# A 3x3 convolution with 2x2 max pooling: two row algorithms on alternate image pairs, in a hand-written order

## The chip, the core and the metric

The kernel runs on one core of a Trainium2 chip. The core has a matrix engine (TensorE, PE in the profile), a vector engine (VectorE, DVE), a scalar engine (ScalarE, ACT), a general engine (GpSimd, POOL), queues that start DMA transfers (SyncE's is SP), an on-chip memory of 128 partitions (SBUF), and the accumulator memory that TensorE writes (PSUM[...]). The metric is device time in microseconds (us), the median of several executions. The profile's span runs from the first instruction to the last and is about 1 us shorter than that time.

## What is computed

The reference convolves 16 images of 64 channels and 64x64 pixels with 128 filters of 3x3, with zeros around the image, and then takes the maximum of each 2x2 block.

```python
batch, c_in, h, w, c_out, k = 16, 64, 64, 64, 128, 3
x_pad = np.pad(x, ((0, 0), (0, 0), (1, 1), (1, 1)))
conv[b, co] += weight[co, ci, kh, kw] * x_pad[b, ci, kh:kh+h, kw:kw+w]
...
output[b, c, i, j] = np.max(conv[b, c, 2*i:2*i+2, 2*j:2*j+2])
```

The output is 16 x 128 x 32 x 32 in fp32. Both kernels multiply in bf16 and accumulate in fp32.

## The kernel before

Two images make a pair: the 64 channels of the first lie on partitions 0 to 63, those of the second on 64 to 127, and the loop runs over eight pairs. An image pair comes in by two DMA transfers of 1 MB (L66, L67), top half and bottom half, and is cast to bf16 into `xpad` with a zero row above and below: the top half by ScalarE (L72), the bottom half by VectorE (L73), the zero rows by GpSimd (L70, L71).

The weights are prepared once. For each of the nine taps, VectorE copies the tap's weights twice side by side (L52, L53), TensorE transposes them in fp32 (L55), and ScalarE casts the result into `wt` (L57), so that the same 64x128 weights lie on both halves of the partitions.

A pair is worked in eight chunks of eight rows. A chunk has two accumulators, `pa` and `pb`, one PSUM bank for each image. For each of the nine taps there are two matmuls, one for each image: L96 uses partitions 0 to 63, L97 uses 64 to 127. I call the two a *pair of matmuls*. A matmul streams 8 x 64 = 512 columns, or 8 x 63 = 504 for a tap at the left or right edge.

Then, for each image, ScalarE copies the accumulator to SBUF (`sb`, L107), VectorE takes the maximum of neighbouring columns (`cm`, L109) and then of neighbouring rows into `oacc` (L113). The output of a pair goes out in two stores of 512 KB from ScalarE's queue (L101, L122). Tile pools and the framework's scheduler set the order; PSUM has three buffers each for `pa` and `pb`.

Of the kernel before, what the change touches and what calls it, by code (L numbers as in the profile page):

```python
# [1 line left out]

# [5 lines left out]


@with_exitstack
def kernel(
    ctx: ExitStack,
    tc: tile.TileContext,
    x: bass.AP,
    weight: bass.AP,
    pool_size: bass.AP,
    out: bass.AP,
):
    nc = tc.nc  # L20
    FP32 = mybir.dt.float32
    BF16 = mybir.dt.bfloat16

    B, CI, H, W = x.shape
    CO, _, K, _ = weight.shape
    assert pool_size == 2
    HP = H + 2
    WP = W + 2
    HO, WO = H // 2, W // 2

    ROWS = 8
    NCHUNK = H // ROWS

    const = ctx.enter_context(tc.tile_pool(name="const", bufs=1))
    wpsum = ctx.enter_context(tc.tile_pool(name="wpsum", bufs=2, space=bass.MemoryType.PSUM))
    psum = ctx.enter_context(tc.tile_pool(name="psum", bufs=3, space=bass.MemoryType.PSUM))
    xraw_pool = ctx.enter_context(tc.tile_pool(name="xraw_pool", bufs=2))
    xpad_pool = ctx.enter_context(tc.tile_pool(name="xpad_pool", bufs=2))
    colmax_pool = ctx.enter_context(tc.tile_pool(name="colmax_pool", bufs=8))
    oacc_pool = ctx.enter_context(tc.tile_pool(name="oacc_pool", bufs=2))  # L40

    ident = const.tile([128, 128], FP32)
    make_identity(nc, ident)

    wraw = const.tile([CO, CI * K * K], FP32)
    nc.sync.dma_start(out=wraw, in_=weight.rearrange("a b c d -> a (b c d)"))  # L46

    wk = []
    for k in range(K * K):
        wdup = const.tile([CO, 2, CI], FP32, name=f"wdup_{k}")  # L50
        src = wraw.rearrange("a (ci k) -> a k ci", k=K * K)[:, k, :]
        nc.vector.tensor_copy(out=wdup[:, 0, :], in_=src)  # L52
        nc.vector.tensor_copy(out=wdup[:, 1, :], in_=src)  # L53
        wp = wpsum.tile([128, 128], FP32, name="wpsum")
        nc.tensor.transpose(wp, wdup.rearrange("a b c -> a (b c)"), ident)  # L55
        wt = const.tile([128, CO], BF16, name=f"wt_{k}")
        nc.scalar.copy(out=wt, in_=wp)  # L57
        wk.append(wt)

    out_v = out.rearrange("b c h w -> c b (h w)")  # L60

    for p in range(B // 2):
        xv = x[2 * p : 2 * p + 2].rearrange("b c h w -> (b c) h w")
        xraw_t = xraw_pool.tile([128, H // 2, W], FP32, name="xraw_t")
        xraw_b = xraw_pool.tile([128, H // 2, W], FP32, name="xraw_b")
        nc.sync.dma_start(out=xraw_t, in_=xv[:, 0 : H // 2])  # L66
        nc.sync.dma_start(out=xraw_b, in_=xv[:, H // 2 : H])  # L67

        xpad = xpad_pool.tile([128, HP, W], BF16)
        nc.gpsimd.memset(xpad[:, 0, :], 0.0)  # L70
        nc.gpsimd.memset(xpad[:, H + 1, :], 0.0)  # L71
        nc.scalar.copy(out=xpad[:, 1 : 33, :], in_=xraw_t)  # L72
        nc.vector.tensor_copy(out=xpad[:, 33 : H + 1, :], in_=xraw_b)  # L73

        oacc = oacc_pool.tile([128, 2, HO * WO], FP32)

        for c in range(NCHUNK):
            y0 = c * ROWS
            pa = psum.tile([128, ROWS, W], FP32, name="pa")
            pb = psum.tile([128, ROWS, W], FP32, name="pb")  # L80
            korder = [1, 4, 0, 3, 6, 2, 5, 8, 7]
            for i, k in enumerate(korder):
                kh, kw = k // K, k % K
                st = i == 0
                sp = i == K * K - 1
                rows = xpad[:, y0 + kh : y0 + kh + ROWS]
                if kw == 1:
                    mv = rows.rearrange("p a b -> p (a b)")
                    oa, ob = pa, pb
                elif kw == 0:  # L90
                    mv = rows[:, :, 0 : W - 1]
                    oa, ob = pa[:, :, 1:W], pb[:, :, 1:W]
                else:
                    mv = rows[:, :, 1:W]
                    oa, ob = pa[:, :, 0 : W - 1], pb[:, :, 0 : W - 1]
                nc.tensor.matmul(oa, wk[k][0:CI, :], mv[0:CI], start=st, stop=sp)  # L96
                nc.tensor.matmul(ob, wk[k][CI:128, :], mv[CI:128], start=st, stop=sp)  # L97

            for half, pt in ((0, pa), (1, pb)):
                if half == 0 and c == 5:  # L100
                    nc.scalar.dma_start(  # L101
                        out=out_v[:, 2 * p : 2 * p + 2, 0 : HO * WO // 2],
                        in_=oacc[:, :, 0 : HO * WO // 2],
                    )
                pv = pt
                sb = colmax_pool.tile([128, ROWS, W], FP32, name=f"sb{half}")
                nc.scalar.copy(out=sb, in_=pv)  # L107
                cm = colmax_pool.tile([128, ROWS, WO], FP32, name=f"cm{half}")
                nc.vector.tensor_tensor(  # L109
                    out=cm, in0=sb[:, :, 0::2], in1=sb[:, :, 1::2],  # L110
                    op=mybir.AluOpType.max,
                )
                nc.vector.tensor_tensor(  # L113
                    out=oacc.rearrange("p b (h w) -> p b h w", h=HO)[
                        :, half, y0 // 2 : y0 // 2 + ROWS // 2, :
                    ],
                    in0=cm[:, 0::2, :],
                    in1=cm[:, 1::2, :],
                    op=mybir.AluOpType.max,
                )  # L120

        nc.scalar.dma_start(  # L122
            out=out_v[:, 2 * p : 2 * p + 2, HO * WO // 2 :],
            in_=oacc[:, :, HO * WO // 2 :],
        )


# [1 line left out]
_INS = ['x', 'weight', 'pool_size']  # L129
_OUTS = [((16, 128, 32, 32), 'float32')]  # L130
#: Inputs that are plain numbers.
_NUMBERS = {'pool_size': 2}


# [26 lines left out]
```

## Time and profile before

| what | value |
|---|---|
| time, median of 3 | 146.98 us (146.45 to 147.07) |
| span of the profile | 145.9 us |
| bytes read, written | 17.07 MB, 8.39 MB |
| mean granted TensorE clock | 0.995 |
| pairs of matmuls in the convolution | 576 |

"Busy" in the profile is the time in which at least one instruction of an engine was under way. A matmul's record is longer than its turn, since the next one starts before it has drained, so two lines of matmuls that run side by side can each show nearly the whole span. What counts for TensorE is the distance between starts.

### The profile page before, as it was taken

Reading aid. Unit: us, or ns where it says so; the run is one execution under the profiler, and the core shown is the slowest. Engines: PE = TensorE matmul, PEld = TensorE weight load, DVE = VectorE, ACT = ScalarE, POOL = GpSimd, SP = SyncE. Lnnn points to the kernel's source line nnn. Section 1 sums busy time; section 2 is a strip of 40 time slices with the busy share of each in tenths; the row PEclk is TensorE's granted clock in tenths of the full one; section 3 lists DMA queues with packets and bytes.
Section 4 is the critical chain, followed back from the end, with each engine's and each line's share of the span. In section 5 each row is a group of like instructions: output and inputs, shape, how many; then the busy total and the mean of one; then the engine's idle time right before and its main releaser. Section 6 shows DMA issues by size and latency. Waiting matters only on the chain.

```text
span 145.9 us, 3022 instructions
## 1 busy us (share of the span) xinstructions
PE 131.7 (90%) x1161; PEld 58.0 (40%) x1161; DVE 95.2 (65%) x282; ACT 86.2 (59%) x146; POOL 8.6 (6%) x22
## 2 busy tenths in 40 slices
PE   0159999999999999999999999999999999999930
PEld 0023344444444444444444444444444444444410
DVE  0630287686768685878679676867686858586770
ACT  3174644578555955597367755695559555463640
POOL 2000000030001200030003000300002000000000
PEclk9999999999999999999999999999999999999997
DMA  5999995308960598139840994030302112030303
GB/s 164 409 427 427 395 332 231 144 2 236 384 247 3 133 344 334 57 63 284 369 152 16 259 408 184 7 146 0 144 4 84 60 67 81 13 131 4 144 0 144
DMA packets 6813, 25.64 MB, mean 176 GB/s; under 512 B 528, under 2 KB 528, under 8 KB 4752
## 3 DMA queue, kind: packets, MB, share of 16 engines
q1 hardware_dynamic: 2448, 17.07, 32.3%
q10 hardware_dynamic: 4352, 8.39, 15.1%
q8 instruction: 9, 0.15, 0.4%
q14 instruction: 4, 0.03, 0.1%
HBM read 17.07 MB, written 8.39 MB: 175 GB/s over the span
## 4 chain that ended last, share of the span: by engine, by line
PE 90%; DMA 4%; ACT 2%; DVE 1%; SPq 0%; issue 0%; ACTq 0%
PE pa L96 86%; DMA xraw_t<-in_x_dram 4%; PE pb L97 2%; PE wpsum L55 2%; ACT xpad L72 1%; DVE cm L109 1%; ACT sb L107 0%; DVE oacc L113 0%; SPq L46 0%; ACT wt L57 0%; ACTq L107 0%
## 5 line engine op out<-in xcount | busy, mean ns | idle before, releaser
L96 PE MATMUL pa<-xpad,wt 64*128 64x504 bf16 (+1 forms) x576 | 127.6, 382 | 0.0
L97 PE MATMUL pb<-xpad,wt 64*128 64x504 bf16 (+1 forms) x576 | 127.6, 382 | 0.0
L96 PEld LDWEIGHTS <-wt 64*128 64x128 bf16 x576 | 54.8, 95 | 70.5 <-issue 3.6
L109 DVE TENSOR_TENSOR cm<-sb 128x256 f32<-128x256 f32 x128 | 53.6, 423 | 35.9 <-ACT sb L107 35.9
L107 ACT COPY sb<-pa 128x512 f32<-128x512 f32 x64 | 37.5, 585 | 46.2 <-PE pb L97 33.0
L97 PEld LDWEIGHTS <-wt 64*128 64x128 bf16 x576 | 54.8, 95 | 0.5 <-issue 0.5
L113 DVE TENSOR_TENSOR oacc<-cm 128x128 f32<-128x128 f32 x128 | 36.8, 292 | 3.9
L107 ACT COPY sb<-pb 128x512 f32<-128x512 f32 x64 | 37.9, 592 | 0.0
L72 ACT CAST xpad<-xraw_t 128x2048 bf16<-128x2048 f32 x8 | 15.3, 1909 | 4.9 <-DMA xraw_t<-in_x_dram 4.9
L70 POOL MEMSET xpad<- 128x64 bf16 x8 | 7.5, 937 | 101.2 <-DVE oacc L113 101.2
L73 DVE CAST xpad<-xraw_b 128x2048 bf16<-128x2048 f32 x8 | 9.8, 1226 | 3.4 <-DMA xraw_b<-in_x_dram 3.4
L55 PE MATMUL wpsum<-ident,wdup 128*128 128x128 f32 x9 | 3.5, 452 | 8.3 <-ACT wt L57 4.2
L71 POOL MEMSET xpad<- 128x64 bf16 x8 | 7.3, 918 | 0.0
L55 PEld LDWEIGHTS wpsum<-ident,wdup 128*128 128x128 f32 x9 | 1.6, 187 | 10.4 <-ACT wt L57 6.2
L52 DVE COPY wdup<-wraw 128x64 f32<-128x64 f32 x9 | 1.9, 209 | 3.7 <-DMA wraw<-in_weight_dram 3.7
L57 ACT CAST wt<-wpsum 128x128 bf16<-128x128 f32 x9 | 2.2, 265 | 3.1 <-PE wpsum L55 3.1
L53 DVE COPY wdup<-wraw 128x64 f32<-128x64 f32 x9 | 1.9, 208 | 0.0
L72 ACT ACT_TABLE_LOAD x1 | 1.3, 1283 | 0.7 <-PEq L142 0.7
masks.py:199 POOL TENSOR_SCALAR_AFFINE_SELECT ident<-ident 128x128 f32<-128x128 f32 x1 | 0.3, 292 | 0.0
masks.py:197 POOL MEMSET ident<- 128x128 f32 x1 | 0.2, 204 | 0.3 <-POOLq L142 0.3
L142 POOL MEMSET const-float32-0.0<- 128x1 f32 x1 | 0.1, 98 | 0.2 <-issue 0.2
L142 POOL MEMSET const-bfloat16-1.0<- 128x1 bf16 x1 | 0.1, 101 | 0.0
(2 smaller groups left out, 0.2 us busy)
## 6 DMA issues: line engine op xcount, KB each, us to landing
xraw_t<-in_x_dram SPq DMA_DIRECT2D x8, 1024.0 KB, 8.5
xraw_b<-in_x_dram SPq DMA_DIRECT2D x8, 1024.0 KB, 7.0
out_dram<-oacc ACTq DMA_DIRECT2D x16, 512.0 KB, 3.1
wraw<-in_weight_dram SPq DMA_DIRECT2D x1, 288.0 KB, 2.9
```

The source lines that it names most:

```text
L52: nc.vector.tensor_copy(out=wdup[:, 0, :], in_=src)
L55: nc.tensor.transpose(wp, wdup.rearrange("a b c -> a (b c)"), ident)
L57: nc.scalar.copy(out=wt, in_=wp)
L70: nc.gpsimd.memset(xpad[:, 0, :], 0.0)
L71: nc.gpsimd.memset(xpad[:, H + 1, :], 0.0)
L72: nc.scalar.copy(out=xpad[:, 1 : 33, :], in_=xraw_t)
L73: nc.vector.tensor_copy(out=xpad[:, 33 : H + 1, :], in_=xraw_b)
L96: nc.tensor.matmul(oa, wk[k][0:CI, :], mv[0:CI], start=st, stop=sp)
L97: nc.tensor.matmul(ob, wk[k][CI:128, :], mv[CI:128], start=st, stop=sp)
L107: nc.scalar.copy(out=sb, in_=pv)
L109: nc.vector.tensor_tensor(out=cm, in0=sb[:, :, 0::2], in1=sb[:, :, 1::2], op=mybir.AluOpType.max,)
L113: nc.vector.tensor_tensor(out=oacc.rearrange("p b (h w) -> p b h w", h=HO)[:, half, y0 // 2 : y0 // 2 + ROWS // 2, :], in0=cm[:, 0::2, :], ...
```

## The change

Both new algorithms compute the two rows of a 2x2 block together, to need fewer products than the six row products (two output rows by three weight rows) of the direct form. Let g0, g1, g2 be the three rows of a filter (each with its three horizontal taps), and x-1, x0, x1, x2 the four input rows under two output rows e and o.

The eight image pairs alternate. On the even ones, "K", there are **five** row products:

- A = (g2-g1) x1 + g0 x-1, B = (g0-g1) x0 + g2 x2, and R = g1 (x0+x1); then e = A + R, o = B + R, so max(e, o) = max(A, B) + R.
- TensorE makes A (step `PA`) and B (`PB`); ScalarE copies A to SBUF (`EV`); VectorE writes max(A, B) over B in PSUM (`MX`); TensorE adds R on top of it (`PR`); ScalarE copies the odd columns (`OD`) and VectorE takes the maximum with the even columns, reading PSUM with a step of two (`CM`). VectorE makes x0+x1 (`KS`).

On the odd ones, "W", there are **four**:

- M = (g0-g1+g2)/2 times (x1-x0), P = (g0+g1+g2)/2 times (x0+x1), g0 (x-1 - x1) and g2 (x2 - x0); e = M + P + g0(..), o = -M + P + g2(..).
- TensorE makes M (`P2`); ScalarE writes -M into a second accumulator (`SE`); TensorE adds g0(..) to the first (`P0`) and g2(..) to the second (`P3`); `ev` and `mx` take the maximum of the two as above; P is added on top (`P1`); `od` and `cm` end it. VectorE makes x0+x1 (`WS`), GpSimd the three differences (`Z`, `Y`, `E`, the first five `E` on VectorE).

A quarter of an image pair (8 pooled rows) is the unit of work, and there are 16 quarters of each kind. Four accumulators of two banks, one for each image, fill PSUM. The K pairs are loaded and cast to bf16 by GpSimd's own DMA queue; the W pairs stay fp32. The weights are combined and transposed in bf16 at the start (steps `T..`, `V..`), and eight matmuls on constants stand ahead of everything. The order of all steps on all engines is written out:

```diff
+    ctx.enter_context(tc.manual_schedule())
+    acc = [psum.tile([128, 2, R, W], FP32, name=f"acc_{i}") for i in range(4)]
...
+    def pa(i):
+        taps(t, D2, step2(kx[j], 2 * q * R + 1), start=True)
+        taps(t, G0, step2(kx[j], 2 * q * R - 1), skip=0 if q == 0 else None)
...
+    def rowmax(g, h=None):
+        t = acc[tb[g]][:, halves(h)]
+        nc.vector.tensor_tensor(out=t, in0=t, in1=ev[g][:, halves(h)], op=MAX)
+    def odd(g, h=None):
+        nc.scalar.copy(out=od[g][:, halves(h)], in_=acc[tb[g]][:, halves(h), :, 1::2])
...
+    def colmax(g, h=None):
+        nc.vector.tensor_tensor(
+            out=o, in0=acc[tb[g]][:, s, :, 0::2], in1=od[g][:, s], op=MAX
+        )
...
+    def on_gpsimd(inst):
+        behind(inst, sbuf_op[0])
...
+    STEADY = """
+        PA+0 OD-1 CM-1 P2+0 mx-1 EV+0 PB+0 SE+0 P1-1 MX+0 P0+0 od-1 P3+0 cm-1 ev+0 PR+0 KS+1
+        WS+1 Z+1 Y+1 E+2
+    """
+    TAIL = """
...
+        ev.15.1 mx.15.1 P1.14 od.14 cm.14 PR.15 OD.15 CM.15 P1.15.0 P1.15.1
+        od.15.0 cm.15.0 od.15.1 cm.15.1
+    """
```

`on_gpsimd` makes each of GpSimd's row operations wait for the last row operation of VectorE (`KS`, `WS`, ...). The last product (`P1.15`), its `od`, `cm` and store are done image by image, the two stores on two queues.

## Prediction

> **What bounds the kernel now.** I read the busy shares first, then the chain of work that ended last, then the costliest groups.
>
> ```profile
> PE 131.7 (90%) x1161; PEld 58.0 (40%) x1161; DVE 95.2 (65%) x282; ACT 86.2 (59%) x146; POOL 8.6 (6%) x22
> ...
> PE 90%; DMA 4%; ACT 2%; DVE 1%; SPq 0%; issue 0%; ACTq 0%
> ...
> L96 PE MATMUL pa<-xpad,wt 64*128 64x504 bf16 (+1 forms) x576 | 127.6, 382 | 0.0
> L97 PE MATMUL pb<-xpad,wt 64*128 64x504 bf16 (+1 forms) x576 | 127.6, 382 | 0.0
> ...
> L109 DVE TENSOR_TENSOR cm<-sb 128x256 f32<-128x256 f32 x128 | 53.6, 423 | 35.9 <-ACT sb L107 35.9
> L107 ACT COPY sb<-pa 128x512 f32<-128x512 f32 x64 | 37.5, 585 | 46.2 <-PE pb L97 33.0
> ```
>
> TensorE is 90% of the span and of the chain; ScalarE and VectorE wait for it. L96 and L97 each show 127.6 us because they run side by side. The timeline gives the pace:
>
> ```profile
> 137.69 0.38 PE L96 MATMUL pa<-xpad,wt 64*128 64x512 bf16 x1
> 137.69 0.38 PE L97 MATMUL pb<-xpad,wt 64*128 64x512 bf16 x1
> ...
> 139.63 0.38 PE L96 MATMUL pa<-xpad,wt 64*128 64x512 bf16 x1
> ...
> 140.10 0.58 ACT L107 COPY sb<-pa 128x512 f32<-128x512 f32 x1 [0.87 <-PE pb L97]
> ```
>
> Nine pairs in 1.94 us: 0.216 us a pair, for 504 columns as for 512. So 576 x 0.216 = 124.4 us. The last turn ends at 139.85; 139.85 - 124.4 = 15.4 us is what the start costs (first weights, input[...]), and 145.9 - 139.85 = 6.05 us is the tail. Also: ScalarE starts 0.25 us after the end of the turn that it waits for.
>
> [...]early pairs stand 0.43 us apart, until about 18 us:
>
> ```profile
> 14.43 0.63 PE L96 MATMUL pa<-xpad,wt 64*128 64x504 bf16 x1
> ...
> 14.86 0.63 PE L96 MATMUL pa<-xpad,wt 64*128 64x504 bf16 x1
> ```
>
> [...]a memset that takes 0.15 us at the start takes 1.20 us beside a 1.23 us cast and ends with it.[...]
>
> ```profile
> 46.77 1.23 DVE L73 CAST xpad<-xraw_b 128x2048 bf16<-128x2048 f32 x1
> 46.89 1.20 POOL L70 MEMSET xpad<- 128x64 bf16 x1 [14.29 <-DVE oacc L113]
> ```
>
> [...]
>
> **The matmuls.** A K quarter has five products of three taps, 15 pairs; a W quarter has 12. So 16 x 27 = 432 pairs, 432 x 0.216 = 93.3 us. In 24 of them one row of eight falls away at an image edge (-0.65 us), and the last product, image by image, runs its three pairs as six single turns (+0.65). Net 93.3 us, 31.1 less than before. I take 0.216 for the row patterns with a step of two as well, since lines of 63 and 64 values already cost the same.
>
> **Prices of the rest.** ScalarE: the 512-value copy has 585 ns, 592 beside it, and a 128-value cast 265, so 0.83 ns a value: 1024 values 1.02 us (`EV`, `SE`, `ev`), 512 values 0.59 (`OD`, `od`). Sum of a round: 3 x 1.02 + 2 x 0.59 = 4.2 us. VectorE: 256 values 423 ns, 128 values 292, so 1.02 ns a value; two in a row stand 0.33 us apart for 256[...]; the full duration I estimate at 1.25 us for `MX`, `mx` and 0.72 for `CM`, `cm`[...]. [...]`WS` 0.59.[...] GpSimd: no two-input operation is in the trace.[...]
>
> TensorE's round is 27 x 0.216 = 5.83 us: every other engine has less work, so TensorE stays the bound if the order lets it.
>
> **Does it?** I walk one round from `STEADY`, t = 0 at `PA`'s start. Turns on TensorE: `PA` 0-1.30, `P2` -1.94, `PB` -3.24, `P1` of the round before -3.89, `P0` -4.54, `P3` -5.18, `PR` -5.83.
> ScalarE: `OD` of the round before waits for `PR`, 0.25 to 0.84; `EV` waits for `PA`, 1.55 to 2.57; `SE` follows, 2.60 to 3.62, and `P0` needs it at 3.89; `od` 4.14 to 4.73; `ev` 4.79 to 5.81.
> VectorE: `CM` 0.88 to 1.60, and `PB`, which reuses its accumulator, needs it at 1.94; `mx` 1.5 to 2.8, `P1` needs it at 3.24; `MX` waits for `PB`, 3.5 to 4.75, `PR` needs it at 5.18; `cm` 4.78 to 5.5, the next `PA` needs it at 5.83; `KS`, `WS` then to 6.3 to 6.6, and the next `CM` wants VectorE at 6.7.
> GpSimd: `Z`, `Y`, `E` from 6.4 to 9.9; the next `KS` is due at 11.2, the next `P0` at 9.7 needs `Z` only.
> Each hand-over has 0.2 to 0.45 us to spare. None is late, so the added work costs nothing per round: TensorE's own turns hide it. Because slack is thin I add 2 us in all for bubbles (0.13 a round).
>
> DMA: loads 17 MB, stores 8.4 MB over 107 us is 238 GB/s; the page shows 427 in a slice. Stores become 1 KB pieces, but a load is issued over a round before its use. Nothing added.
>
> **The start.** The weights arrive at 3.7 us as now (the first VectorE copy starts at 3.68). Two subtractions (0.26 us apart), four transposes, a PSUM copy, a cast of the first rows (0.4 each) and the transposes of three more blocks lead to `PA.0` at about 6.2 us[...]. The eight constant matmuls run until about 4.2, before the weights can be used, and cost nothing. Then come the waits: `P2.0` waits for the transposes behind `PA.0`, and `PA.1` for the cast `X1` or `X2`, which stand behind `EV.0` and `SE.0` on ScalarE. Walking it the same way, the first two quarters (51 pairs, 11.0 us) end at about 20.7: the start costs 9.7 us, against 15.4. Bounds: 8.2 if `PA.1` needs only `X1`[...].
>
> **The tail.** From the last turn's end: 0.25, a 256-value `od` for each image (the second ends 0.65 later, since the first runs under the second's matmuls), a `cm` of 0.42, then the store. Before, the store from its issue at 142.16 to the end took 3.7 us for 512 KB; for 128 KB I take 3.1, between that and the 2.9 that the 288 KB weight load took to land. 4.5 us against 6.05.
>
> **Sum:** 9.7 + 93.3 + 2 + 4.5 = 109.5 us of span, plus the 1.1 between span and time: **110.6**, I say 110.5.
>
> **Rivals.** (1) *Hand-overs eat the slack.* If the copies and the signals between engines take 0.3 us more than I assume, `SE` and `CM` pass their due times, and a round grows by some 0.5 us: + 8, 118.5 us. For it: seven hand-overs a round with at most 0.45 us each. Against: ScalarE to VectorE takes 0.04 us here (140.685 to 140.72).
> (2) *Strided PSUM reads at half rate.* `OD` 1.02, `CM` 1.25 us: `CM` ends at 2.6, `PB` is 0.7 late, and `cm` ends at 7.2, so a round is 7.2: + 1.4 x 15 = 21, 131 us.[...] Against: `cm` at L109 reads SBUF with a step of two at the full 1.02 ns.
> (3) *GpSimd becomes the bound.* At 1.75 us each, 5.25 + 1.4 (`KS`, `WS`, signals) = 6.65: + 0.8 x 13 rounds, 121 us. **Slower than before** it gets from about 2.5: at 2.6 us, 7.8 + 1.4 = 9.2, + 3.4 x 13 = 44, 154.6 us. The wait that `on_gpsimd` adds puts GpSimd and VectorE's `KS`, `WS` in a ring, and behind `KS` all of VectorE's queue stands, `CM` first, and so `PB`.[...]
> (4) *Everything fits,* the better start and no bubbles: 107.
>
> **Chances.** Forecast 0.60 (108 to 114), rival 1 0.16, rival 2 0.07, rival 3 mild 0.06, severe 0.03, rival 4 0.08. From 106 to 119 the first two and the fourth are held, some 0.82. Faster takes all but the severe one and a share for something unforeseen: 0.96; same 0.01; slower 0.03.
>
> **What would show it.** TensorE's pairs 0.216 us apart through `PA`, `P2`, `PB`; the same step 5.83 to 6.0 us apart from round to round; `PA.0` near 6.2 us; `MX` 1.25, `OD` 0.59, GpSimd's operations 1.2 us; TensorE about 85% busy. The prediction is wrong if rounds stand 6.5 us apart or more: then the wait ahead of `PB` or `PA` (rival 2), of `P0` (rival 1) or of VectorE's `KS` (rival 3) says which.

## The result and the profile after

The changed kernel takes **108.13 us** (median of four runs, 107.96 to 108.97), the kernel before on the same chip 146.74 (146.45 to 147.07). The ratio is **0.737, with a 95% interval of 0.734 to 0.741**. The forecast was 110.5 us with a range of 106 to 119. All ratios below are to the kernel before, on the chip of that experiment; of the runs of a kernel, those more than 1.5% above its fastest are left out of its ratio. The kernels of experiments 1, 2, 4 and 6 were timed once.

In the views below, L185 is every matmul of the convolution, and what it reads tells the step: `kx` for `PA` and `PB`, `ks` for `PR`, `we` for `P2`, `wz` for `P0`, `wy` for `P3`, `ws` for `P1`. L250 holds the row operations (`KS`, `WS`, `Z`, `Y`, `E`), L292 `EV` and `ev`, L301 `SE`, L305 `MX` and `mx`, L310 `OD` and `od`, L324 `CM` and `cm`, L333 the stores, L340 and L347 the casts of the first rows.

The page of the changed kernel answers the first lines of the prediction: busy time, the chain by engine, then the costliest groups of VectorE, ScalarE and GpSimd (busy time, mean ns of one, and after the second bar the idle time before them and what ended most of it).

```profile
PE 98.7 (93%) x900; PEld 51.2 (48%) x900; DVE 82.3 (78%) x115; ACT 72.3 (68%) x92; POOL 60.6 (57%) x70
...
PE 84%; DVE 6%; DMA 4%; ACT 1%; issue 1%; SPq 0%; ACTq 0%; DVEq 0%
...
L305 DVE TENSOR_TENSOR acc<-acc,ev 128x1024 f32<-128x1024 f32 (+1 forms) x34 | 39.5, 1166 | 11.9 <-PE acc L185 11.4
...
L292 ACT COPY ev<-acc 128x1024 f32<-128x1024 f32 (+1 forms) x34 | 32.6, 964 | 12.5 <-PE acc L185 11.0
L250 POOL TENSOR_TENSOR wz<-wx 128x512 bf16<-128x512 f32 x16 | 20.3, 1271 | 30.3 <-DVE ws L250 24.3
```

TensorE's busy time fell by 33 us, from 131.7 to 98.7, and the span by nearly 40, from 145.9 to 106.2: most of it is matmuls that are no longer made (31.7 us of turns, worked out below), the rest is nearly all at the start (15.4 us before, 7.1 now). Which part of the new start brings these us was not tested, apart from the constants (experiments 7 and 8). TensorE still carries most of the chain. GpSimd's busy time rose from 8.6 to 60.6 us, VectorE now waits mostly for TensorE, and GpSimd's `Z` waits for `ws`, which is the wait that `on_gpsimd` adds.

The chain in order of time (start, length, what) shows that TensorE hardly stops between the first and the last quarter, and what stands at both ends:

```profile
1.19 4.27 DMA kfirst<-in_x_dram
...
5.96 1.39 PE acc L185 x12
...
9.64 81.42 PE acc L185 x756
...
100.07 0.85 PE acc L185 x6
...
101.80 0.37 ACTq L333
...
102.21 0.38 ACT od L310
...
102.61 0.42 DVE o L324
```

From 9.64 to 91.06 us the chain has one entry: 378 pairs in 81.42 us, 0.2154 us each, with no wait long enough to break it. Ahead of `PA.0` stands the load of the first input rows, not the weights. At the end the two halves come one after the other: the second `od` (102.21) starts only after the issue of the first store (ACTq, 101.80), and the last `cm` ends at 103.03.

The timeline of one steady round (start, length, engine, line; in square brackets the idle time before it and its cause) can be laid beside the walk of the prediction:

```profile
52.86 1.40 PE L185 MATMUL acc<-kx,wt 64*128 64x512 bf16 x12
...
53.70 0.69 DVE L324 TENSOR_TENSOR o<-acc,od 128x512 f32<-128x512 f32 x1 [0.32 <-ACT od L310]
...
54.29 1.01 ACT L292 COPY ev<-acc 128x1024 f32<-128x1024 f32 x1 [0.63 <-PE acc L185]
...
54.73 1.48 PE L185 MATMUL acc<-kx,wt 64*128 64x512 bf16 x12
...
55.34 1.01 ACT L301 ACTIVATE acc<-acc 128x1024 f32<-128x1024 f32 x1
...
56.67 0.83 PE L185 MATMUL acc<-wz,wt 64*128 64x512 bf16 x6
...
58.62 1.48 PE L185 MATMUL acc<-kx,wt 64*128 64x512 bf16 x12
```

`PA` starts at 52.86, the next at 58.62: 5.76 us, in a round in which `PA` lacks an image row at the edge (its turn is 1.22 us); the round after it took 5.83. (A matmul group's length here, 0.83 or 1.40 to 1.48 us, includes its drain; the turns are 0.65 and 1.3 us.) The slack of each hand-over is the gap between the end of a step and the start of the turn that needs it. `CM` ends at 53.70 + 0.69 = 54.39 and `PB` starts at 54.73: 0.34. `SE` ends at 56.35 and `P0` starts at 56.67: 0.32. Further on, `MX` ends at 57.53 and `PR` starts at 57.97: 0.44. TensorE's bracket is empty at each of these turns.

### The profile page after: what moved, and what is told of

Its sections match the earlier page's. It is cut to its first block, busy times and chain, and to the rows that moved or that the text cites. A ratio compares the mean times of both kernels' runs of the same rounds, so it can differ in the third digit from the quotient of the medians.

```text
span 106.2 us, 2337 instructions
## 1 busy us (share of the span) xinstructions
PE 98.7 (93%) x900; PEld 51.2 (48%) x900; DVE 82.3 (78%) x115; ACT 72.3 (68%) x92; POOL 60.6 (57%) x70
## 4 chain that ended last, share of the span: by engine, by line
PE 84%; DVE 6%; DMA 4%; ACT 1%; issue 1%; SPq 0%; ACTq 0%; DVEq 0%
PE acc L185 83%; DVE acc L305 5%; DMA kfirst<-in_x_dram 4%; PE acc L151 1%; DVE o L324 1%; ACT od L310 1%; DVE kx L340 0%; SPq L105 0%; ACTq L333 0%; DVEq L305 0%
## 5 line engine op out<-in xcount | busy, mean ns | idle before, releaser
L185 PEld LDWEIGHTS <-wt 64*128 64x128 bf16 x864 | 48.6, 94 | 45.1 <-issue 1.8
L305 DVE TENSOR_TENSOR acc<-acc,ev 128x1024 f32<-128x1024 f32 (+1 forms) x34 | 39.5, 1166 | 11.9 <-PE acc L185 11.4
L185 PE MATMUL acc<-kx,wt 64*128 64x504 bf16 (+3 forms) x384 | 46.6, 373 | 0.6 <-DVE kx L340 0.6
L292 ACT COPY ev<-acc 128x1024 f32<-128x1024 f32 (+1 forms) x34 | 32.6, 964 | 12.5 <-PE acc L185 11.0
L250 POOL TENSOR_TENSOR wz<-wx 128x512 bf16<-128x512 f32 x16 | 20.3, 1271 | 30.3 <-DVE ws L250 24.3
L310 ACT COPY od<-acc 128x512 f32<-128x512 f32 (+1 forms) x33 | 19.0, 574 | 12.5 <-PE acc L185 11.5
L324 DVE TENSOR_TENSOR o<-acc,od 128x512 f32<-128x512 f32 (+1 forms) x33 | 22.1, 674 | 4.5 <-ACT od L310 4.4
L250 POOL TENSOR_TENSOR wy<-wx 128x512 bf16<-128x512 f32 x16 | 20.3, 1270 | 0.0
L301 ACT ACTIVATE acc<-acc 128x1024 f32<-128x1024 f32 x16 | 16.1, 1008 | 1.0 <-PE acc L185 0.5
L250 POOL TENSOR_TENSOR we<-wx 128x512 bf16<-128x512 f32 x11 | 14.1, 1278 | 0.1
L185 PE MATMUL acc<-ws,wt 64*128 64x504 bf16 (+1 forms) x96 | 13.3, 377 | 0.4 <-DVE acc L305 0.4
L185 PE MATMUL acc<-ks,wt 64*128 64x504 bf16 (+1 forms) x96 | 13.3, 377 | 0.1
L185 PE MATMUL acc<-we,wt 64*128 64x504 bf16 (+1 forms) x96 | 13.3, 377 | 0.0
L185 PE MATMUL acc<-wz,wt 64*128 64x504 bf16 (+1 forms) x96 | 13.2, 377 | 0.0
L185 PE MATMUL acc<-wy,wt 64*128 64x504 bf16 (+1 forms) x96 | 13.2, 377 | 0.0
L250 DVE TENSOR_TENSOR ws<-wx 128x512 bf16<-128x512 f32 x16 | 10.9, 684 | 0.0
L250 DVE TENSOR_TENSOR ks<-kx 128x512 bf16<-128x512 bf16 x16 | 6.7, 417 | 0.0
L250 DVE TENSOR_TENSOR we<-wx 128x512 bf16<-128x512 f32 x5 | 3.6, 722 | 0.1
```

The source lines that it names most:

```text
L185: nc.tensor.matmul(dst[:, half, i0:i1, o0:o1], wt[lo : lo + CI, m0 + kw - half, :], rows(lo, i0, i1, c0, c1), start=start and kw == 1, sto ...
L250: return engine.tensor_tensor(out=row_out(name, i), in0=row_in(t, f + a, pad), in1=row_in(t, f + b, pad), op=op)
L292: nc.scalar.copy(out=ev[g][:, halves(h)], in_=acc[ta[g]][:, halves(h)])
L301: nc.scalar.mul(acc[t], acc[ta["w", i]], -1.0)
L305: nc.vector.tensor_tensor(out=t, in0=t, in1=ev[g][:, halves(h)], op=MAX)
L310: nc.scalar.copy(out=od[g][:, halves(h)], in_=acc[tb[g]][:, halves(h), :, 1::2])
```

## The experiments

**1. The last step of a W quarter left out.** Theory: TensorE sets the round, but other chains stand close behind it. The rival is that TensorE alone counts.

```diff
     def p3(i):
-        taps(tb["w", i], G2, step1(row["wy", i // NQ], i % NQ))
+        pass
```

> Leaves out P3, one of the four products of the odd image pairs (3 of 27 turns of a round, 16 times), so the odd pairs' output is not the reference's. Theory (TensorE is the bound, but the hand-overs have only 0.3 to 0.4 us to spare): without P3 the stretch from P1's end to the next PA is 1.30 us instead of 1.95, and od, cm and their signals need 0.25 + 0.59 + 0.04 + 0.69 + 0.04 = 1.61, so each round loses 0.65 of turns and gets 0.3 to 0.5 of waiting: 5.4 to 5.6 us a round, 102 to 105 us in all. Rival A (TensorE's turns alone set the time, slack is ample): 16 x 0.65 = 10.4 us less, 97.7 us. Rival B (another engine already sets the round): no change, 108.

Measured: 106.13 us. A full round, from `PA` at 58.89 us to the next at 64.35, is 5.46 us, where TensorE's turns alone would give 5.83 - 0.65 = 5.18. The end of this round in the timeline:

```profile
62.40 1.23 DVE L305 TENSOR_TENSOR acc<-acc,ev 128x1024 f32<-128x1024 f32 x1 [0.86 <-PE acc L185]
...
62.77 0.83 PE L185 MATMUL acc<-wz,wt 64*128 64x512 bf16 x6
...
63.61 0.69 DVE L324 TENSOR_TENSOR o<-acc,od 128x512 f32<-128x512 f32 x1
...
63.69 0.82 PE L185 MATMUL acc<-ks,wt 64*128 64x512 bf16 x6
```

Two chains now end together. `MX` ends at 63.63 and `PR` starts at 63.69, 0.92 us after `P0` instead of 0.65: here TensorE waits 0.27 us. `cm` ends at 64.30 and `PA` starts at 64.35. From the end of `P1`'s turn at 62.77 to `PA` it is 1.58 us, where the theory had 1.61. So the theory holds in size, and `cm` is as close as it says; but the wait in which most of the time is lost is that of `PR` for `MX`, which it didn't name. The total is above the theory's range because of the start, not the rounds: the first input landed late, `PA.0` began at 6.86 instead of 5.96, and its six pairs then took 2.58 us instead of 1.39. From `PA.2` to `PB.15` it took 73.3 us, against 77.6 in the changed kernel.

**2. The same products in a plain order.** The steady part runs each quarter through all its steps before the next one, K and then W, with the same operations.

```diff
-    for i in range(FIRST, LAST + 1):
-        for s in STEADY.split():
-            steps[s[:-2]](i + int(s[-2:]))
-    run(TAIL)
...
+    PLAIN = """
+        PA+0 EV+0 PB+0 MX+0 PR+0 OD+0 CM+0 P2+0 SE+0 P0+0 P3+0 ev+0 mx+0 P1+0 od+0 cm+0
+        KS+1 WS+1 Z+1 Y+1 E+2
+    """
...
```

> The same work, but from quarter 4 on in plain order: one K quarter from start to end, then one W quarter, no product of another quarter in between. Theory (the hand-written order hides the hand-overs under TensorE's turns): TensorE waits for MX (1.6 us), for SE (1.3) and for ev and mx (2.0) in every round, which goes from 5.8 to about 10.6 us: 12 rounds x 4.8 = 58 us more, some 160 to 170 us, slower than the kernel before. Rival (the smaller number of matmuls brings the gain, the order little): under 118 us.

Measured: 169.63 us, slower than the kernel before with its 576 pairs. The page and the timeline of this kernel:

```profile
PE 107.8 (64%) x900; PEld 49.5 (29%) x900; DVE 83.4 (50%) x112; ACT 72.3 (43%) x89; POOL 60.5 (36%) x70
```

```profile
61.11 0.82 PE L185 MATMUL acc<-ks,wt 64*128 64x512 bf16 x6 [1.39 <-DVE acc L305]
...
63.74 0.82 PE L185 MATMUL acc<-wz,wt 64*128 64x512 bf16 x6 [1.16 <-ACT acc L301]
...
66.94 0.82 PE L185 MATMUL acc<-ws,wt 64*128 64x512 bf16 x6 [1.73 <-DVE acc L305]
```

The same 900 matmuls, but TensorE stands still three times a round: before `PR` for `MX`, before `P0` for `SE`, before `P1` for `mx`. That is 1.39 + 1.16 + 1.73 = 4.28 us, and three times some 0.17 us of drain that no next turn covers (0.82 - 0.65): 5.83 + 4.28 + 0.5 = 10.6; measured from this `PR` to the next at 71.67, 10.56. The written order is what turns fewer matmuls into less time. (An order made by the framework's scheduler was not tried.)

**3. GpSimd without the ordering wait.** The wait that ties GpSimd's row operations behind VectorE's `KS` and `WS` is taken out. Is it a cost, or does it protect something?

```diff
     def on_gpsimd(inst):
-        behind(inst, sbuf_op[0])
```

> GpSimd's row operations no longer wait for VectorE's last row operation (a wait for order only, no data). Theory: GpSimd is ahead, its operations then fall beside KS and WS, which have two inputs in SBUF; VectorE's KS and WS grow from 0.42 and 0.68 to 1.2 us or more, they end after the next CM is due (0.33 us to spare), PB waits, and the rounds with such a clash grow by 0.3 to 0.9 us: 110 to 118 us. Rival (the two engines do not hinder each other, the wait is idle): KS and WS as before, 108.1 within 0.4 us, or faster.

Measured: 117.18 us (116.76 to 119.33), ratio 0.797 (0.792 to 0.802); so the wait saves 9 us. (The edit also frees the weights' sum `GS` at the start; `PA.0` began at 6.21 us, 0.25 later than in the changed kernel.) The timeline of this kernel (its line 249 is the 250 of the others), an undisturbed `KS` first, then a later round:

```profile
46.64 0.41 DVE L249 TENSOR_TENSOR ks<-kx 128x512 bf16<-128x512 bf16 x1
...
58.45 1.28 POOL L249 TENSOR_TENSOR wz<-wx 128x512 bf16<-128x512 f32 x1
...
58.85 1.17 DVE L249 TENSOR_TENSOR ks<-kx 128x512 bf16<-128x512 bf16 x1
...
59.67 1.47 POOL L249 TENSOR_TENSOR wy<-wx 128x512 bf16<-128x512 f32 x1
59.94 1.75 DVE L249 TENSOR_TENSOR ws<-wx 128x512 bf16<-128x512 f32 x1
```

`KS` starts at 58.85 under a GpSimd `Z` that ends at 59.73, and ends 0.29 us after it: 1.17 us instead of 0.41. `WS` starts under `Y`, which ends at 61.14, and ends at 61.69: 1.75 us instead of 0.68. Both are VectorE operations with two SBUF inputs beside a GpSimd operation that reads SBUF, a case that the trace of the kernel before did not have. GpSimd's operation can grow too: `Y` took 1.47 us here, where it takes 1.27 in the changed kernel. Behind `WS` stands `CM` in VectorE's queue, and behind `CM` the next `PB`: TensorE waited for `o` (`CM`) six times, 7.3 us in all, of the 8.6 us by which the stretch from `PA.0` to the last product grew.

```profile
PE acc L184 <- DVE o L323: 7.3, 6, 1.8
```

**4. Two more GpSimd operations a round.** Two row differences that nothing uses are added, to see where GpSimd becomes the bound, which was rival 3.

```diff
+        on_gpsimd(row_op(nc.gpsimd, "xz", i, -1, 1, SUB))
+        on_gpsimd(row_op(nc.gpsimd, "xy", i, 2, 0, SUB))
```

> Two more differences a quarter on GpSimd (copies of Z and Y that nobody reads), each behind VectorE's last row operation as the others. Theory (GpSimd's operations and VectorE's KS and WS exclude each other, so they form a ring): 5 x 1.23 + 1.1 + 0.2 = 7.4 us a round instead of 5.8, and KS waits, behind it CM, and so PB: some 13 rounds x 1.6 = 21 us more, 127 to 133 us. Rival (GpSimd's own work alone counts): 5 x 1.23 = 6.15, + 0.4 x 13 = 5 us, 113 us.

Measured: 130.78 us. Nearly all steady rounds took 7.0 to 7.2 us, or 7.4 where GpSimd also issues a load (0.58 us). Total and rounds are about as expected, the place not: TensorE waited at `P3` for `Y`, fourteen times, 19.3 us in all, and not at `PB`. In the timeline:

```profile
50.98 1.28 POOL L250 TENSOR_TENSOR wz<-wx 128x512 bf16<-128x512 f32 x1 [0.64 <-DVE ws L250]
...
56.00 0.83 PE L185 MATMUL acc<-wy,wt 64*128 64x512 bf16 x6 [1.41 <-POOL wy L250]
56.15 2.17 DVE L250 TENSOR_TENSOR ws<-wx 128x512 bf16<-128x512 f32 x1
```

This is the ring: `Z` waits for `WS` (50.98), the four operations behind it follow, and the last of them, `E`, ends at 57.76; the next `WS`, beside it, starts at 56.15 and ends at 58.32, 0.56 us after `E`; the next `Z` starts at 58.40, 7.42 us after the first. The changed kernel has the same ring with three operations instead of five, and there it has room: in the round shown further up, `E` ends at 57.27 and the next `KS` starts at 58.11.

**5. and 6. A delay on ScalarE.** A copy that nothing uses stands behind each `EV` of a K quarter, ahead of `SE`; of 192 values in one kernel, of 768 in the other. This asks how much slack `SE` has before `P0`, and whether rival 1 is far.

```diff
...
+        if g[0] == "k":
+            nc.scalar.copy(out=idle[:, 0:192], in_=idle_in[:, 0:192])
```

> An idle ScalarE copy of 192 values (SBUF to SBUF, nobody reads it) behind every EV of the K quarters, so ahead of SE: some 0.3 us more in ScalarE's queue a round. Theory (SE ends 0.32 us before P0 needs it, so the hand-over absorbs it): from PA.0 to the last product 94.1 to 94.8 us as in the control (94.1), 108.1 to 109 us in all. Rival (the order is tight everywhere, any work more is paid in full): + 16 x 0.3 = 4.8 us, 113 us.

> The same copy with 768 values: some 0.75 us more ahead of SE. Theory: 0.32 us of it is absorbed, 0.4 to 0.5 us a round is not, and P0 waits for SE: + 6 to 8 us, 114.5 to 116.5 us. Rival A (ScalarE has 28% idle time, so it is absorbed): 108.5. Rival B (paid in full): + 12 us, 120.5.

The short copy lasts 0.356 us and runs 17 times (the last `EV` is done in two halves), 6.1 us of added work. The kernel took 108.73 us (108.53 to 108.86), ratio 0.739 (0.736 to 0.742). In the traces, the time from the start of `PA.0` to the start of the last product grew by 0.5 us, from 94.1 to 94.6, in the first and the last quarters; the steady rounds kept their 5.76 and 5.83 us, so there the copy was absorbed. The long copy lasts 0.836 us, and TensorE waited at each `P0` for `SE`; in the timeline of one round (here L296 is `EV`, L307 `SE`, L298 the added copy, which starts at 60.94):

```profile
60.03 1.01 ACT L296 COPY ev<-acc 128x1024 f32<-128x1024 f32 x1 [0.63 <-PE acc L185]
...
61.67 1.01 ACT L307 ACTIVATE acc<-acc 128x1024 f32<-128x1024 f32 x1
...
62.74 0.82 PE L185 MATMUL acc<-wz,wt 64*128 64x512 bf16 x6 [0.16 <-ACT acc L307]
```

The steady rounds took 6.09 to 6.17 us, 0.33 to 0.41 more. How much slack is that? The added copy delays `SE` by less than its own length: it starts 0.10 us before `EV` has ended, and `SE` 0.10 us before the copy has, while in the changed kernel `SE` starts 0.04 us after the end of `EV`. From the start of `EV` to that of `SE` it is 1.05 us in the changed kernel (54.29 to 55.34), 1.16 with the short copy and 1.64 with the long one. So the short copy moved `SE` by 0.11 us only, within the 0.32 us that lie between the end of `SE` and `P0`; the long one moved it by 0.59 us and `P0` by 0.33 (62.74, where `P1`'s turn had ended at 62.41). The slack on this path is therefore some 0.26 us; the other 0.06 remain between `SE`'s end at 62.68 and `P0` even when TensorE waits. The total, 117.04, is 0.5 above the range of the theory; here too the first input came late (`PA.0` at 7.17), and its six pairs took 2.26 us instead of 1.39.

**7. and 8. Without the matmuls on constants.** The eight matmuls ahead of everything are removed. The W load that waited for the fourth of them waits for a GpSimd memset instead, so that it starts at about the same time (issued at 2.38 us instead of 2.68). The second kernel is the same, run beside an unaltered copy of the changed kernel (the control).

```diff
...
-    for n in range(8):
-        warm = nc.tensor.matmul(
-            acc[n // 2][:, n % 2], ones[:, 0:128], ones, start=True, stop=True, skip_group_check=True
-        )
-        if n == 3:
-            behind(wload(0), warm)
+    behind(wload(0), last_memset)
```

> The eight matmuls on constants left out; the load wx(0) that waited for the fourth now waits for the last GpSimd memset of the weights' buffer, at about the same time. Theory[...]: PA.0 and what follows stand 0.43 us apart[...], 1.5 to 2.5 us lost: 109.6 to 110.6 us. Rival ([...]the start waits for VectorE and ScalarE anyway): within 0.4 us of 108.1.

> The changed kernel itself, unaltered, on the same chip as the three beside it, as the yardstick for differences under 1%: 108.0 to 108.6 us.

> The run without the eight constant matmuls again, now beside a control on the same chip, since the arrival of the first input differs by up to 1 us between the runs so far. Theory[...]: PA.0's six pairs and the next stand 0.43 us apart until about 11 us; 1.5 to 3.5 us slower than the control. Rival (the late input alone made e3 slow): within 0.4 us of the control.

The first of the two took 111.48 us (109.6 to 111.52). Its trace is of one of three runs at 111.5; `PA.0` came at 7.15 us, late, and the time from there to the last product was 96.46 us instead of 94.11. The fourth run took 109.6, and no control ran beside it, so this 2.35 us stays the figure of one trace and is not used further. Beside the control, 108.5 us (108.22 to 108.73), ratio 0.737 (0.734 to 0.740), the second took 109.64 us (108.8 to 110.42), ratio 0.746 (0.742 to 0.751): 1.1 us more, less than expected. The timeline of the second, its transposes and the six pairs of `PA.0`:

```profile
4.29 1.86 PE L151 MATMUL acc<-ident,wq 128*128 128x128 bf16 x16 [4.29 <-DVE wq L354]
...
6.25 1.94 PE L185 MATMUL acc<-kx,wt 64*128 64x512 bf16 x12
```

Six pairs in 1.94 us, against 1.39 in the changed kernel: 0.55 us lost, and the rest of this run is as long as in the control (94.66 - 94.11 = 0.55). This trace is of the fastest of the four runs. So the constants buy 0.55 us in this trace and 1.1 in the medians; why the other runs lost more was not traced. The constants don't always succeed: in experiment 1, which has them, TensorE stood idle for 1.39 us ahead of `PA.0` and then took 2.58 us for its six pairs, and in experiment 6 it took 2.26 after 1.93 us; after 0.88 us, in experiment 10, it took 1.39.

**9. and 10. The tail.** In one kernel the last product, its `od`, `cm` and store are done whole. In the other the product is whole, and the two `od` come ahead of the two `cm` on both queues, so that no `od` stands behind a store (the first and the second added order below).

```diff
-        ev.15.1 mx.15.1 P1.14 od.14 cm.14 PR.15 OD.15 CM.15 P1.15.0 P1.15.1
-        od.15.0 cm.15.0 od.15.1 cm.15.1
+        ev.15.1 mx.15.1 P1.14 od.14 cm.14 PR.15 OD.15 CM.15 P1.15 od.15 cm.15
...
+        ev.15.1 mx.15.1 P1.14 od.14 cm.14 PR.15 OD.15 CM.15 P1.15
+        od.15.0 od.15.1 cm.15.0 cm.15.1
```

> Undoes one part of the change: the last product, its od, cm and store for both images at once (P1.15 od.15 cm.15), the rest as it is. Theory (image by image gains nothing: the two images' matmuls run side by side anyway, and od of the second image stands behind the first's store on ScalarE's queue until 102.2): P1.15 ends as before at 100.7, od 0.59, cm 0.69 end at 102.25 instead of 103.03, and the store of 256 KB takes 0 to 0.4 longer than one of 128 KB: 0.4 to 0.8 us faster than the control. Rival (image by image pays, since the first image's od, cm and store run under the second's): 0.3 to 1 us slower than the control.

> P1.15 for both images, then od.15.0, od.15.1, cm.15.0, cm.15.1, so that no store stands ahead of an od. Theory: the second cm ends at 102.1 to 102.4 instead of 103.03, both stores stay at 128 KB: 0.6 to 0.9 us faster than the control, and at least as fast as the whole one. Rival (the order on ScalarE's queue is not what holds the second image): equal to the control.

Whole: 107.69 us (107.39 to 108.25), ratio 0.732 (0.728 to 0.735). Reordered: 107.76 us (107.4 to 108.56), ratio 0.733 (0.728 to 0.737). The intervals overlap with the control's, but the end of the traces does not depend on when the first input arrived: from the start of the last product to the end of the span it is 6.1 us in the changed kernel and in the control, 5.6 whole and 5.5 reordered. The whole tail in the timeline:

```profile
100.03 0.82 PE L185 MATMUL acc<-ws,wt 64*128 64x512 bf16 x6 [0.39 <-DVE acc L305]
...
100.89 0.59 ACT L310 COPY od<-acc 128x512 f32<-128x512 f32 x1 [0.63 <-PE acc L185]
101.51 0.69 DVE L324 TENSOR_TENSOR o<-acc,od 128x512 f32<-128x512 f32 x1 [0.34 <-ACT od L310]
```

The last `cm` ends at 102.20, 2.17 us after the product's start; in the changed kernel at 103.03, 2.96 us after it. Of these 0.8 us 0.3 are lost again, since the whole store takes longer (3.4 us from the last `cm` to the end, against 3.2). Going image by image costs half a microsecond. These two are the fastest kernels of this study, by 0.4 us below the changed kernel's median and 0.7 to 0.8 below the control's.

**11. The first load on another queue, with the tail reordered.** Meant: the first input starts from ScalarE's queue instead of SyncE's, and the two last stores change queues.

```diff
-    nc.sync.dma_start(out=kfirst, in_=rows_of(0, 0, khi))
+    nc.scalar.dma_start(out=kfirst, in_=rows_of(0, 0, khi))
...
-        store = nc.scalar if h == 0 else nc.sync
+        store = nc.sync if h == 0 else nc.scalar
```

> The reordered tail, and the first input rows (kfirst) loaded from ScalarE's queue at the start, instead of behind the weights on SyncE's (issue at 0.7 instead of 1.2 us); the first image's last store from SyncE's queue and the second's from ScalarE's. Theory: the tail is 0.55 us shorter as in the run before, PA.0 starts up to 0.4 us earlier, as far as the weights (ready at 5.2) let it: 107.2 to 107.7 us, against 108.1 to 108.5. Rival (the input then takes bandwidth from the weights, which land later): the start gains nothing, 107.7 to 108.2.

Measured: 123.3 us (121.62 to 124.05), ratio 0.832 (0.824 to 0.840). The edit did more than it was meant to: whole stores have no `h`, so the second line moved all 31 of them to ScalarE's queue. On the tail it therefore says nothing. It shows what a store in that queue costs, in the timeline:

```profile
63.77 0.69 DVE L324 TENSOR_TENSOR o<-acc,od 128x512 f32<-128x512 f32 x1 [1.05 <-ACT od L310]
...
64.49 0.38 ACTq L333 DMA_DIRECT2D out_dram<-o  x1
...
64.91 1.01 ACT L292 COPY ev<-acc 128x1024 f32<-128x1024 f32 x1 [1.18 <-PE acc L185]
```

The store waits for `CM`, which ends at 64.46, and `EV`, queued behind the store, starts only then, although ScalarE had been idle for 1.18 us: the bracket names TensorE, but the queue shows the store. The steady rounds took 6.41 us instead of 5.76 to 5.83. The first load gained nothing either: the weights were there at 5.57 us instead of 3.71, and `PA.0` started at 7.72. A kernel with a better start and the whole tail was not tried.

Nor was one algorithm alone on all pairs, so that no run shows what alternating them is worth. An estimate from the durations above: two W quarters would be 24 x 0.216 = 5.2 us of turns, but six GpSimd operations of 1.23 us, 7.4; two K quarters would be 30 x 0.216 = 6.5 us of turns, against 5.83.

## Why the prediction was right, and where it was off

The time is 2.4 us below the forecast, 2%. Of the span, 3.3 us is missing; the profiled execution has 1.8 us outside its span (107.97 - 106.2), where 1.1 was assumed. (The 1.1 set the span of one execution of the kernel before against a median of others; its runs beside the experiments have 1.8 as well, such as 147.11 us with a span of 145.3.)

| term | predicted | measured in the changed kernel |
|---|---|---|
| start | 9.7 | 7.1: the first 51 pairs end at 18.09, less the same 11.0 |
| matmuls | 93.3 | 92.7: 432 x 0.216, less 0.65 for the edge rows |
| bubbles | 2 | 0.9: 0.26 ahead of the last `PR` but one, 0.57 ahead of the last product |
| tail | 4.5 | 5.5: 106.2 - 100.72, the end of the last turn |
| span | 109.5 | 106.2 |
| outside the span | 1.1 | 1.8 |

That the sum came within 2% is in part luck: three terms were too high, by 4.3 us in all, and two too low, by 1.7. The measured time lies nearer to rival 4 (a better start, no bubbles: 107) than to the forecast.

- **The bound.** Right. TensorE sets every steady round, 5.76 and 5.83 us against 5.83; with 0.65 us of turns taken out, experiment 1 has full rounds of 5.46, so the next chains stand only 0.37 us behind.
- **The walk of a round.** Right to 0.1 us at each turn: `P0` was placed 3.89 us after `PA` and starts at 3.81, `PB` 1.94 and 1.87, `PR` 5.18 and 5.11; the difference is the row that `PA` lacks in this round. The slack was put at 0.2 to 0.45 us a hand-over, and the trace has 0.32 to 0.44 in the three above. Experiments 5 and 6 measured 0.26 for one of them, the 0.32 of `SE`, by using it up. The 2 us for bubbles was caution that the walk didn't ask for: the steady rounds have next to none, and the 0.9 us stand in the last two.
- **Prices.** `MX` 1.23 us for 1.25, `CM` 0.69 for 0.72, `OD` 0.59 for 0.59, GpSimd 1.27 for 1.2. `WS` took 0.68 for 0.59, `KS` 0.42. The trace of the kernel before has no VectorE operation on PSUM and no two-input operation of GpSimd: 1.25, 0.72 and 1.2 were the author's estimates, and on them rested that these two engines have less work in a round than TensorE. (The 423 ns for 256 values and 1.02 ns a value would give `MX` 1.21 and `CM` 0.68 us; for GpSimd that trace gives nothing.) With the durations measured, a round has 4.9 us of VectorE and 3.8 of GpSimd, against TensorE's 5.83. In the group view of the changed kernel:

```profile
L310 ACT COPY od<-acc 128x512 f32<-128x512 f32 x31 | 18.2, 587 | 10.9 <-PE acc L185 10.9
L324 DVE TENSOR_TENSOR o<-acc,od 128x512 f32<-128x512 f32 x31 | 21.2, 690 | 3.5 <-ACT od L310 3.5
```

- **Rival 2, strided PSUM reads,** falls with these two lines: 587 ns for `OD` with a step of two, 585 for the contiguous copy of the same size before.
- **Rival 1** did not happen, but is near: 0.26 us more on one path is what the order has to spare (experiment 6).
- **Rival 3** did not happen, because GpSimd's operation takes 1.27 us and because the ordering wait keeps it out of VectorE's way. The prediction saw the wait as a risk only, the ring behind `KS`. Experiment 3 shows that it is worth 9 us.
- **The start: mis-sized, 2.6 us too much.** `PA.0` was put at 6.2 and came at 5.96, but on another path: the prediction walked the weights and transposes, while the chain runs through the load of the first input rows, which landed at 5.46. Two steps failed behind it. The first is the pace of the first pairs. The author's estimate had them 0.43 us apart until perhaps 8 us, as the early pairs of the kernel before are until about 18; that is worth some 0.9 us (1.8 us at 0.43 a pair instead of 0.216). `PA.0` ran at full pace at once, six pairs in 1.39 us. The eight matmuls on constants were costed at nothing, which is right (TensorE waited 0.41 us for the weights after them), and also credited with nothing, which is not: experiment 8 puts them at 0.55 us in the trace and 1.1 in the medians. The prediction did not ask what the 3.17 us of constants ahead of everything do to the pace of the first pairs; how much of them it takes, and by what means they act, no run shows. The second is the wait of `PA.1`. The timeline of the changed kernel has the casts `X1` and `X2` and, between them, `PA.1`:

```profile
9.33 0.63 ACT L347 CAST kx<-ksecond 128x512 bf16<-128x512 f32 x1
...
10.23 1.46 PE L185 MATMUL acc<-kx,wt 64*128 64x512 bf16 x12
...
11.41 0.61 ACT L347 CAST kx<-ksecond 128x512 bf16<-128x512 f32 x1
```

`PA.1` needs `X1` only, so that neither the second cast nor `SE.0` ahead of it counts. The prediction had this case as its lower bound, 8.2; the start came out 1.1 us below even that, and where this last part lies was not tested.

- **The split of the last product: mis-sized, 0.65 us too much.** Six single turns were to take twice the time of three pairs. In the trace they start in pairs all the same, six in 0.83 us, as in any steady turn.
- **The tail: mis-sized, 1 us too little.** The step that failed is "the first runs under the second's matmuls". Both halves of the product waited until the second image's `mx` ended at 100.02, although the first image's had ended at 99.21, so there was nothing for the first `od` to run under; and the second `od` then stood behind the store in ScalarE's queue until 102.21. The store itself, from the last `cm`'s end at 103.03 to 106.2, took 3.2 us against 3.1.

In the traces, the spread among runs comes from the arrival of the first input. `PA.0` started between 5.88 and 7.17 us in the changed kernel, the control and experiments 5, 6, 9 and 10, whose first loads are the same. From there to the last product it took 94.10 to 94.15 us in the four of them without a delay. That may also be part of why the medians in experiments 9 and 10 differ from the control's by more than the tail gives; only one run of each was traced.

## What to carry to other kernels

An algorithm with fewer products is worth what the order lets it be worth: the same operations gave 108 us in an order with a few tenths of slack at each hand-over, and 170 in a plain one. Walk one round with the measured durations, note the slack of each hand-over, and look at what else stands in the queue of the engine that hands over: here a store ahead of `EV` made rounds of 6.41 us out of 5.76 to 5.83, and a `WS` that took 1.75 us beside GpSimd instead of 0.68 held up the `CM` behind it. A wait that looks like a cost can be protection (here 9 us), and only taking it away tells.

## What the runs showed of the hardware

- ScalarE's read of every second fp32 value of PSUM was as fast as a contiguous one (587 and 585 ns for 512 values).
- The six matmuls of the last product, which the program writes as three on one half of the partitions and then three on the other, started in pairs, six in 0.83 us, as when they are written alternately. Whether TensorE's queue held them in the written order the trace doesn't tell.
- VectorE operations with two SBUF inputs took longer beside a GpSimd operation that reads SBUF: 0.41 us became 1.17, and 0.68 became 1.75 (experiment 3) and 2.17 (experiment 4). The GpSimd operation beside the 1.75 took 1.47 us instead of 1.27. `MX`, which reads one input from PSUM and one from SBUF, kept its 1.22 us beside GpSimd operations of 1.28 (changed kernel, at 54.30).
- Matmuls on constants ahead of the work bought 0.55 us in one trace and 1.1 in the medians (experiment 8). An idle stretch of 1.39 or 1.93 us ahead of the first real matmul was followed by a slow start (experiments 1 and 6: 2.58 and 2.26 us for six pairs), one of 0.88 us was not (experiment 10: 1.39).
- A ScalarE copy of 0.836 us, put between two others, delayed the second of them by 0.59 us, one of 0.356 us by 0.11 (experiments 5 and 6).
- With the same first loads, the first product started up to 1.3 us apart from run to run (5.88 to 7.17 us).
